# The low parts of the weights in the first block's two mixers: from GpSimd and VectorE to VectorE alone

## The chip, the cores and the metric

The kernel runs on one core of one Trainium2 chip. The metric is the device time of one execution in microseconds (us); lower is better. Engines are named as the profile does: PE is TensorE, DVE is VectorE, ACT is ScalarE, POOL is GpSimd, SP is SyncE, from which the loads are issued.

## The reference

Two transformer blocks of two layers each run one after the other over 256 tokens of width 1024, in float32. The change lies in the first block, whose two layers each have a mixer (attention, gated linear attention, a convolution branch) and a feed-forward part. In layer 0 the mixer runs over 512 columns (the context and the latent tokens), in layer 1 over the 256 latent tokens for most of its projections. Cut to what matters:

```python
def _latent_mixer(h, mem, cos, sin, p):
    proj = h @ p['w_in']                       # 9760 columns: k v kg vg glr | q qg r glu gates
    ...
    o_att = _attend_blocks(_apply_rope(q, cos, sin), k_all, v_all)
    o_gla, _, _ = _gla_bidir(qg, kg, vg, gf, gb, s_f, s_b)
    return _merge(o_att, o_gla, r, glu, gates, p)

def _conv_module(glu, p):                      # depthwise, 31 taps, over 1024 channels
    a, g = jnp.split(glu, 2, axis=-1)
    y = a * jax.nn.sigmoid(g)
    y = lax.conv_general_dilated(y, p['conv_w_dw'], ...) + p['conv_b_dw']
    y = jax.nn.silu(_layernorm(y, p['conv_ln_g'], p['conv_ln_b']))
    return y @ p['w_conv_o']

def _merge(o_att, o_gla, r, glu, gates, p):
    y_att = o_att... @ p['w_att_o']
    y_gla = (rmsnorm(o_gla) * jax.nn.silu(r)) @ p['w_gla_o']
    y_conv = _conv_module(glu, p)
    g_att, g_gla, g_conv = jnp.split(jax.nn.sigmoid(gates), 3, axis=-1)
    return (g_att * y_att + g_gla * y_gla + g_conv * y_conv) @ p['w_out']
```

## The kernel before

**Products in three matmuls.** Weights and activations are float32; the matmuls run on a shorter type. Each operand is split into a high part (the value rounded to that type) and a low part (the value minus the high part), and a product is the sum of three matmuls: high x high, low x high, high x low. For weights `wsplit` does this, tile by tile: ACT casts the loaded tile `raw` to `whi` (L362), and one elementwise subtraction gives `wlo` (recorded at L288, the line of the helper `tt`). A tile is 128 x 1024 values: eight k steps of 128 output columns (`fm`, used by `mm_fm`, L386 to L388), or two k steps of 512 columns (`proj_tm`, used by `mm_tm`, L467 to L469). The third matmul of a k step in `mm_fm` (L388), the second in `mm_tm` (L468), reads `wlo`. `whi` and `wlo` have three buffers each, `raw` two.

**Who subtracts.** `wsplit` counts its calls and sends the subtraction to POOL on every `self.pool_lo`-th call, otherwise to DVE; 0 means always DVE:

```python
on_pool = self.pool_lo and self.nsplit % self.pool_lo == 0
after = self.lo_behind.pop() if self.lo_behind else None
with self.tc.issue_after(after.ins) if after else nullcontext():
    self.tt(lo, src, hi.bitcast(F32), ALU.subtract, self.nc.gpsimd if on_pool else None)
```

`mixer` sets `pool_lo` at its start from `PLO0` (layer 0) or `PLO1` (layer 1), first entry, and again behind the attention's output projection, second entry. The second entries are 0 already. So the first entry rules: the conv branch's projections `a` and `g`, the projections k/v, q, the gate rank `glr`, kg, qg, in layer 1 also vg, and the first merge (its gates and `w_att_o`). `opening` (the first tiles of `a` and `g`), `post`, `hold` and `prehold` choose POOL by rules of their own.

**What runs beside it.** The convolution is 30 `scalar_tensor_tensor` operations on DVE for each of eight channel tiles, after one `tensor_scalar` (`conv`, tiles `ca`, L291): over both layers 480. They are generated in the background, in pairs of channel tiles, at 1.6 (layer 0) or 1.0 (layer 1) steps of four operations per weight tile, and with priority `CP` = 600, behind everything else, while the split of a weight tile has -100 (`WP`). Their sums `cs` are added up on POOL. The result is first read by `conv_norm`, at the head of the second merge. DVE also multiplies the conv gate (`gt`), normalises q and k heads (`qn`, `ra`, `rb`), and does the softmax's maximum and scaling and the low parts of activations (`s`, `P`, `PT`, `lo`); POOL raises small tiles to the power -1/2 (`s`).

**Order.** A planner orders the instructions of every engine ahead of time by priority and readiness; on the chip each engine runs its own list in order.

Of the kernel before, what the change touches and what calls it, by code (L numbers as in the profile page):

```python
# [28 lines left out]
GRATE0 = 0.8  # L29
GRATE1 = 0.6  # L30
CP = 600
PLO0A = 1
PLO0B = 0
PLO0 = PLO0A, PLO0B
PLO1A = 2
PLO1B = 0
PLO1 = PLO1A, PLO1B
NW = 8
# [2144 lines left out]
```

## Time and profile before

| | |
|---|---|
| runs | 2651.34, 2652.18, 2655.23 us; median 2652.18 us |
| profiled execution | 2647.99 us, of it 2646.2 us span |
| PE busy | 2442.5 us (92%) |
| DVE busy | 1710.3 us (65%) |
| ACT busy | 1118.7 us (42%) |
| POOL busy | 786.7 us (30%) |
| low parts of weights on DVE, on POOL | 357, 115 |

The profile is of one execution. A busy share is an average over stages; a stage is read from its own windows. "idle before, releaser" says how long an engine stood before an instruction and whose end released it. Matmuls are pipelined: their durations overlap, and starts tell the pace. The granted clock is TensorE's, as a share of 2.4 GHz.

### The profile page before, as it was taken

What the parts mean: (1) busy time and instruction counts of PE and PEld (TensorE: products, weight loads), DVE (VectorE), ACT (ScalarE), POOL (GpSimd) and SP (SyncE); (2) the same over time, 40 slices, a digit from 0 to 9 for tenths busy, and PEclk for the clock granted to TensorE, in tenths of its full rate; (3) what the DMA queues carried; (4) which work ended last, traced back from release to release, by engine and by line L of the source; (5) the groups of instructions that cost most, each with busy time, mean ns of one, the idle gap of its engine ahead of it and who ended that gap; (6) DMA issues with size and microseconds to landing.
All of it is one profiled execution on the core that took longest, in us unless ns stands there. A gap on an engine that the chain in (4) does not pass through costs nothing. (4 is left out here: it accounts for less than half of the span.)

```text
span 2646.2 us, 38822 instructions
## 1 busy us (share of the span) xinstructions
PE 2442.5 (92%) x15227; PEld 2089.7 (79%) x15227; DVE 1710.3 (65%) x2803; ACT 1118.7 (42%) x2063; POOL 786.7 (30%) x554
## 2 busy tenths in 40 slices
PE   7768889989999899999987998898999999999998
PEld 5556678777887777876886888887997989888997
DVE  5768997898345733343699879967654556546664
ACT  3113336644343422122343574554453544446443
POOL 2775531577002400101543125714035010112001
PEclk9889899999999999999989999999999999999999
DMA  7323211222334245355243224444574446653454
GB/s 245 128 70 114 64 52 48 80 65 80 112 128 159 85 142 188 113 190 199 83 125 98 67 88 123 132 138 140 175 241 127 128 131 207 202 160 101 148 185 157
DMA packets 277690, 345.41 MB, mean 131 GB/s; under 512 B 12894, under 2 KB 208888, under 8 KB 277508
## 3 DMA queue, kind: packets, MB, share of 16 engines
q1 hardware_dynamic: 277508, 342.94, 40.1%
q8 instruction: 120, 1.97, 0.3%
q14 instruction: 62, 0.51, 0.1%
HBM read 341.85 MB, written 1.05 MB: 130 GB/s over the span
## 5 line engine op out<-in xcount | busy, mean ns | idle before, releaser
L388 PE MATMUL pm<-hi,wlo 128*128 128x256 f32 (+1 forms) x2824 | 912.6, 324 | 31.7 <-POOL wlo L288 17.8
L386 PE MATMUL pm<-hi,whi 128*128 128x256 f32 (+1 forms) x2824 | 921.6, 328 | 11.8 <-ACT whi L362 4.2
L387 PE MATMUL pm<-lo,whi 128*128 128x256 f32 (+1 forms) x2824 | 915.2, 325 | 2.4 <-DVE lo L288 1.4
L362 ACT CAST whi<-raw 128x1024 fp32r<-128x1024 f32 (+1 forms) x464 | 484.7, 1048 | 895.0 <-PE pm L387 518.4
L288 DVE TENSOR_TENSOR wlo<-raw,whi 128x1024 fp32r<-128x1024 f32 (+1 forms) x357 | 452.3, 1270 | 355.7 <-ACT whi L362 355.3
L388 PEld LDWEIGHTS pm<-hi,wlo 128*128 128x128 f32 x2824 | 543.7, 193 | 75.3 <-POOL wlo L288 19.5
L386 PEld LDWEIGHTS pm<-hi,whi 128*128 128x128 f32 x2824 | 542.9, 193 | 55.8 <-ACT whi L362 6.7
L387 PEld LDWEIGHTS pm<-lo,whi 128*128 128x128 f32 x2824 | 544.4, 193 | 50.1 <-issue 7.4
L288 POOL TENSOR_TENSOR wlo<-raw,whi 128x1024 fp32r<-128x1024 f32 (+2 forms) x115 | 353.6, 3085 | 419.8 <-ACT whi L362 386.0
L291 DVE SCALAR_TENSOR_TENSOR ca<-gt,cw,ca 128x482 f32<-128x482 f32 (+29 forms) x480 | 331.6, 746 | 0.0
L468 PE MATMUL pm<-wlo,hi 128*128 128x512 f32 x536 | 216.1, 403 | 25.1 <-POOL wlo L288 25.1
L467 PE MATMUL pm<-whi,hi 128*128 128x512 f32 x536 | 217.3, 405 | 13.2 <-ACT whi L362 6.5
L469 PE MATMUL pm<-whi,lo 128*128 128x512 f32 x536 | 214.2, 400 | 0.0
L288 POOL TENSOR_TENSOR hl<-hr,hh 128x512 fp32r<-128x512 f32 (+1 forms) x38 | 54.8, 1444 | 470.1 <-ACT hh L454 321.4
L288 POOL TENSOR_TENSOR s<-s,mhalf 128x1 f32<-128x1 f32 (+2 forms) x82 | 68.1, 831 | 378.8 <-DVE s L295 375.2
L468 PEld LDWEIGHTS pm<-wlo,hi 128*128 128x128 f32 x536 | 103.9, 194 | 49.7 <-POOL wlo L288 28.2
L467 PEld LDWEIGHTS pm<-whi,hi 128*128 128x128 f32 x536 | 104.1, 194 | 39.8 <-ACT whi L362 7.3
L469 PEld LDWEIGHTS pm<-whi,lo 128*128 128x128 f32 x536 | 103.8, 194 | 22.2 <-DVE lo L291 0.4
L288 POOL TENSOR_TENSOR hl<-raw,hh 128x512 fp32r<-128x512 f32 x24 | 35.9, 1515 | 234.5 <-ACT hh L432 232.2
L288 POOL TENSOR_TENSOR eq<-B 128x256 f32<-128x256 f32 x96 | 89.7, 953 | 28.8 <-DVE lo L288 15.9
L467 PE MATMUL pm<-hh,hi 128*128 128x512 f32 (+2 forms) x258 | 92.6, 362 | 5.9 <-ACT hh L432 3.3
L288 POOL TENSOR_TENSOR ek<-B 128x256 f32<-128x256 f32 (+1 forms) x100 | 95.6, 975 | 3.9 <-PE ps L1209 2.0
(327 smaller groups left out, 3470.8 us busy)
## 6 DMA issues: line engine op xcount, KB each, us to landing
raw<-in_w_in_dram SPq DMA_DIRECT2D x84, 1024.0 KB
aw<-in_w_ada_dram SPq DMA_DIRECT2D x192, 256.0 KB
raw<-in_w_gate_up_dram SPq DMA_DIRECT2D x40, 1024.0 KB
raw<-in_w_ff_gate_dram SPq DMA_DIRECT2D x21, 1024.0 KB
raw<-in_w_ff_up_dram SPq DMA_DIRECT2D x21, 1024.0 KB
raw<-in_w_down_dram SPq DMA_DIRECT2D x20, 1024.0 KB
raw<-in_w_ff_down_dram SPq DMA_DIRECT2D x18, 1024.0 KB
raw<-in_w_att_o_dram SPq DMA_DIRECT2D x8, 1024.0 KB
```

Source lines behind the costliest of these rows:

```text
L288: return (eng or self.nc.vector).tensor_tensor(out=out, in0=a, in1=b, op=op)
L291: return self.nc.vector.scalar_tensor_tensor(out=out, in0=a, scalar=s, in1=b, op0=op0, op1=op1)
L362: self.nc.scalar.copy(hi, src)
L386: mm(out, lhsT=hi[:, k, :], rhs=a.hi[k], start=(first and k == 0), stop=False)
L387: mm(out, lhsT=hi[:, k, :], rhs=a.lo[k], start=False, stop=False)
L388: mm(out, lhsT=lo[:, k, :], rhs=a.hi[k], start=False, stop=(last and k == nk - 1))
L467: f(p, lhsT=a.hi[kk][:, sl], rhs=hi, start=first, stop=False)
L468: f(p, lhsT=a.hi[kk][:, sl], rhs=lo, start=False, stop=False)
L469: return f(p, lhsT=a.lo[kk][:, sl], rhs=hi, start=False, stop=last)
```

## The change

Two constants. In the first part of layer 0's mixer every weight tile had its low part made by POOL, in that of layer 1 every second one; now DVE makes all of them.

```diff
-PLO0A = 1
+PLO0A = 0
 PLO0B = 0
 PLO0 = PLO0A, PLO0B
-PLO1A = 2
+PLO1A = 0
 PLO1B = 0
 PLO1 = PLO1A, PLO1B
```

## Rows read from the trace of the kernel before

**Rows 1.** The page, span in 40 slices (tenths): PE busy, granted clock.

```profile
PE   7768889989999899999987998898999999999998
...
PEclk9889899999999999999989999999999999999999
```

**Rows 2.** Waits of PE from 53 to 482 us: total, times, longest.

```profile
PE pm L468 <- POOL wlo L288: 22.3, 3, 16.3
PE pm L388 <- POOL wlo L288: 15.3, 2, 12.9
```

**Rows 3.** Windows behind these waits: length, busy PE PEld DVE ACT POOL, granted clock.

```profile
110.60:114.60 4.00, 3.97 (x9) 3.13 (x10) 0.00 (x0) 0.00 (x0) 4.00 (x2) 0.50 0.75 212
170.00:176.00 6.00, 6.00 (x14) 4.74 (x15) 0.00 (x0) 0.00 (x0) 4.55 (x2) 0.50 0.44 132
90.40:97.00 6.60, 6.60 (x22) 5.28 (x23) 6.60 (x11) 0.00 (x0) 6.60 (x1) 0.74 0.00 0
196.60:199.00 2.40, 2.40 (x6) 1.92 (x7) 0.00 (x0) 0.00 (x0) 2.40 (x2) 0.50 0.52 113
```

**Rows 4.** Timeline of POOL, low parts in mixer 0: start, us.

```profile
118.73 2.39 POOL L288 TENSOR_TENSOR wlo<-raw,whi 128x1024 fp32r<-128x1024 f32 x1 [3.50 <-ACT whi L362]
124.18 2.39 POOL L288 TENSOR_TENSOR wlo<-raw,whi 128x1024 fp32r<-128x1024 f32 x1 [3.05 <-ACT whi L362]
...
75.56 14.78 POOL L288 TENSOR_TENSOR wlo<-raw,whi 128x1024 fp32r<-128x1024 f32 x1 [4.93 <-ACT whi L362]
...
90.30 20.28 POOL L288 TENSOR_TENSOR wlo<-raw,whi 128x1024 fp32r<-128x1024 f32 x1
...
142.61 27.29 POOL L288 TENSOR_TENSOR wlo<-raw,whi 128x1024 fp32r<-128x1024 f32 x1 [2.40 <-ACT whi L362]
...
340.42 2.39 POOL L288 TENSOR_TENSOR wlo<-raw,whi 128x1024 fp32r<-128x1024 f32 x1 [7.86 <-ACT whi L362]
```

**Rows 5.** Timeline of DVE, convolution taps in mixer 0 and mixer 1.

```profile
71.30 16.83 DVE L291 SCALAR_TENSOR_TENSOR ca<-gt,cw,ca 128x482 f32<-128x482 f32 x26
88.05 2.84 DVE L288 TENSOR_TENSOR adar<-adar,ab 4x512 f32<-4x512 f32 x1
...
340.50 2.85 DVE L291 SCALAR_TENSOR_TENSOR ca<-gt,cw,ca 128x500 f32<-128x500 f32 x1
...
1384.96 8.18 DVE L291 SCALAR_TENSOR_TENSOR ca<-gt,cw,ca 128x241 f32<-128x241 f32 x21
```

**Rows 6.** POOL's low parts by line, 53 to 482 us and 1310 to 1625 us.

```profile
L288 POOL TENSOR_TENSOR wlo<-raw,whi 128x1024 fp32r<-128x1024 f32 (+1 forms) x49 | 188.8, 3866 | 185.7 <-ACT whi L362 175.3 <-PE pm L388 10.3
...
L288 POOL TENSOR_TENSOR wlo<-raw,whi 128x1024 fp32r<-128x1024 f32 (+1 forms) x29 | 78.7, 2713 | 133.2 <-ACT whi L362 117.3 <-DMA raw<-in_w_att_o_dram 7.9 <-ACT hTh L302 5.9
```

**Rows 7.** DVE by line: 53 to 482 us, then 1310 to 1650 us.

```profile
L291 DVE SCALAR_TENSOR_TENSOR ca<-gt,cw,ca 128x482 f32<-128x482 f32 (+14 forms) x240 | 193.5, 861 | 0.0
...
L291 DVE SCALAR_TENSOR_TENSOR ca<-gt,cw,ca 128x241 f32<-128x241 f32 (+14 forms) x240 | 138.1, 631 | 0.0
L288 DVE TENSOR_TENSOR wlo<-raw,whi 128x1024 fp32r<-128x1024 f32 x36 | 44.4, 1234 | 11.3 <-ACT whi L362 11.3
```

**Rows 8.** Windows of mixer 0's first part: busy PE PEld DVE ACT POOL, clock.

```profile
53.00:188.00 135.00, 99.50 (x426) 75.33 (x425) 88.98 (x123) 26.20 (x37) 93.87 (x17) 0.85 0.33 108
188.00:300.00 112.00, 90.54 (x376) 67.85 (x375) 92.94 (x144) 32.09 (x110) 61.04 (x28) 0.88 0.27 87
300.00:410.00 110.00, 98.32 (x513) 83.80 (x512) 98.52 (x155) 40.22 (x92) 41.97 (x17) 0.97 0.19 58
```

**Rows 9.** Timeline of DVE: mixer 0's last tap, the first use of the sums.

```profile
386.97 1.75 DVE L291 SCALAR_TENSOR_TENSOR ca<-gt,cw,ca 128x482 f32<-128x482 f32 x1
...
496.81 3.07 DVE L288 TENSOR_TENSOR ca<-ca,ps 128x512 f32<-128x512 f32 x5
```

**Rows 10.** Waits of PE from 1310 to 1650 us (mixer 1, first part).

```profile
PE pm L388 <- DVE wlo L288: 11.9, 4, 4.9
...
PE pm L388 <- POOL wlo L288: 2.6, 3, 1.8
```

**Rows 11.** DVE's low parts from 482 to 760 us: min/median/max ns.

```profile
L288 DVE TENSOR_TENSOR wlo<-raw,whi x39: 1199/1225/1673, 485.4 to 755.3; 128x1024 fp32r<-128x1024 f32 x39
```

## The prediction

> **What bounds the kernel now.** I read the page first. TensorE is busy for most of the span, and its slices stand at 8 or 9 almost everywhere; the weak ones are among the first eight, where the granted clock dips to 8 as well [rows 1]. That is the first part of mixer 0, where all low parts are POOL's. So I asked for TensorE's waits between 53 and 482 us, from the first of these low parts to the last. The two longest entries by far are matmuls that wait for a `wlo` made by POOL: 22.3 us at L468 and 15.3 us at L388, 37.6 us together [rows 2]. The windows behind these waits show the second cost: TensorE comes back at a granted clock of 0.50 (1.2 GHz) and stays there for some microseconds [rows 3].
>
> Why is POOL late? Alone, one 128x1024 low part takes it 2.39 us, and two follow each other at 5.45 us, TensorE's pace for one 128-column weight tile, as the first two rows of [rows 4] show. But other ones of the same form last 14.78, 20.28 and 27.29 us [rows 4]. VectorE's timeline shows what runs beside the first of these: 26 convolution taps back to back, 71.3 to 88.1 us [rows 5]. POOL's instruction is issued at 75.56 and ends at 90.34, 2.2 us after the chain, about what it needs alone, and VectorE's next instruction, a small addition, lasts 2.84 us meanwhile; under the chain POOL made no visible progress. The reverse is in the rows too: a tap that meets a POOL low part issued just before it (340.42) takes 2.85 us [rows 5], against 16.83 / 26 = 0.65 in the chain. So POOL and VectorE exclude each other here, and a chain without gaps keeps POOL out to its end. In total 49 low parts of mixer 0 cost POOL 188.8 us where 49 x 2.39 = 117 would do, and the 29 of mixer 1 cost 78.7 [rows 6].
>
> The Trainium skill ("SBUF — State Buffer", section "Who interferes with whom") states that a VectorE instruction with two SBUF inputs and a GpSimd instruction that reads SBUF take turns by an exclusive lock held for a whole instruction. The 2.85 us tap agrees. Read as a lock of one instruction only, it would have POOL wait one tap (0.65) and end after about 3 us; the 27.29 us row says otherwise, and by that reading the 37.6 us below would not be there to gain. The sum goes by the rows.
>
> **The change part by part.**
>
> *Removed, mixer 0.* POOL's 49 low parts up to `self.pool_lo = ...[1]`. TensorE's waits for them: 37.6 us [rows 2]. The clock behind them: 4.0 + 6.0 + 2.4 us at 0.50 lose half, 6.2 us, and 6.6 us at 0.74 lose 0.26 of it, 1.7 us [rows 3]; 7.9 in all. Together 45.5 us. These waits end the idle of TensorE itself, and right after them TensorE runs without a gap, so I count them in full.
>
> *Added, mixer 0.* 49 low parts on VectorE at 1.23 us (the mean of the 36 that VectorE makes in and just behind mixer 1 [rows 7]): 60 us of VectorE. What hides them? VectorE is busy 89.0 + 92.9 + 98.5 = 280.4 us of the 357 us from 53 to 410 [rows 8]. It also loses what the exclusion costs: the 240 taps take 193.5 us [rows 7], 240 x 0.65 = 156 without POOL, so 37.5 us come back, up to what POOL's few remaining operations there still take. 280.4 + 60.3 - 37.5 = 303 us, in a stretch that shrinks to 357 - 45.5 = 311.5. It fits, with little to spare, and the taps may slip: the last one ends near 388 and the first instruction that needs the finished sums runs at 496.8 [rows 9], so over 100 us of cover, some 60 after the stage has shrunk.
>
> *The price of the new neighbours.* VectorE's queue is in order: a low part now stands behind whatever taps, gate products, head norms or softmax steps were placed ahead of it, and what waits for it is a later matmul of the same k step, with all of TensorE behind. Before shows this on both sides. In mixer 1, where VectorE makes half of them beside the taps, TensorE waits 11.9 us for them [rows 10], over 36 [rows 7]: 0.33 us each, 16 us for 49. In the second part of mixer 0 VectorE makes 39 [rows 11] with no taps beside them, and no wait of TensorE names them: 0. Mixer 0's first part has the taps of the former, but the 512-column matmuls, and so the double cover per weight tile, of the latter. I take the middle, 8 us, and keep 0 and 16 for the range.
>
> *Mixer 1.* 29 low parts leave POOL: 2.6 us of TensorE's waits go [rows 10]. VectorE gets 29 x 1.23 = 35.7 us more, and gives up the tap time lost to POOL: 138.1 - 240 x 0.39 (8.18 / 21 [rows 5]) = 44.5 us. That nearly cancels. By 0.33 us each the new low parts would cost TensorE 9.6 us; but the old ones were themselves late behind VectorE work that POOL held up. Between -15 (both kinds of wait gone) and +7 (9.6 less 2.6) I take 0.
>
> *Not touched.* ScalarE still makes all high parts, the DMA queue issues the same loads from SP, `post`, `hold` and `prehold` set POOL by themselves. POOL keeps the conv sums and the small powers, and finds its way free for them.
>
> *Sum.* -45.5 + 8 + 0 = -37.5 us on the profiled execution's 2648.0 us, 2610.5. That execution lies 4.2 us under the median of the three runs, 2652.2; on the median the forecast is **2614.7, say 2615 us**.
>
> **Rivals.**
>
> *Long chains ahead of a low part (slower).* If the order on VectorE puts chains such as the 26 taps of [rows 5] ahead of a `wlo`, the stall is only moved. There are three `wlo` buffers, one in use, so a low part can be two weight tiles ahead: 2 x 5.45 = 10.9 us of cover, 17 taps. A 26-tap chain of 16.83 us overruns it by 5.9 us, plus some 2.5 us of low clock: 8.4 each. Two such chains for each of the four tap pairs make 67 us, 2652 - 45.5 + 67 = 2674. It decides from six chains on (6 x 8.4 = 50). For it: VectorE's chains are that long now. Against: the taps are given a priority 700 steps behind the low parts, and enter the program at 1.6 x 4 = 6.4 per weight tile, 4.2 us. Chance 0.11.
>
> *VectorE becomes the bound.* If the exclusion gives nothing back (POOL's other work meets the taps as often), the stage holds 280.4 + 60.3 = 341 us of VectorE against 311.5 us of TensorE, and 29 of the 45.5 us are lost: 2652 - 16 = 2636. For it: VectorE is busy 98.5 of 110 us from 300 to 410 [rows 8]. Against: 49 of the POOL operations that meet the taps are the ones that go. The Trainium skill ("Perfetto Trace Analysis", section "Optimizing Scalar/DVE Operations") has the rule on this side, that a saturated VectorE may hand work even to GpSimd, and adds that the two share a port, so that it might not help; [rows 5] speak for the second half. Chance 0.13.
>
> *Mixer 1 gains too.* VectorE loses there 44.5 us to POOL and gets 35.7; if TensorE's 11.9 us for late low parts shrink with the POOL operations that held VectorE, and mixer 0's new waits stay near 0, another 8 (new waits) and 9 us or so (mixer 1) go: about 2598. Chance 0.13.
>
> *The stall only changes its name.* TensorE, no longer held by POOL, meets the taps, the head norms or the softmax at the same places, and the stage ends when it ended: 2652. Against: the waits of [rows 2] are ended by POOL alone, and the taps have 100 us in hand. Chance 0.05.
>
> **How the numbers follow.** The forecast, 2603 to 2632, has 0.58 (its own bounds: 0 and 16 for the new waits, and some microseconds either way for mixer 1). A measurement of this kernel tells about 0.2%, 5.3 us, from no change. Forecast, mixer 1 and VectorE-bound lie below that: 0.84 faster; 0.05 the same; 0.11 slower. The range 2594 to 2645 leaves out about 0.05 below, and the no-change and slower cases, 0.16, above.
>
> **What the profile after would show.** Right: no `wlo` on POOL between 53 and the end of mixer 0's first part, no TensorE wait there of over 10 us, clock 9 or more in the first eight slices, 49 and 29 more low parts on VectorE at about 1.2 us, taps at a mean near 0.7 in place of 0.86, and this stage about 40 us shorter with the rest of the kernel unchanged in length. Wrong: waits of TensorE for `wlo` from VectorE over 20 us (chains), a VectorE without gaps and conv sums finished late, so that TensorE waits at the head of the `w_conv_o` stage (bound), or equal waits under other names.

## The result and the profile after

The changed kernel takes 2571.38 us (median of 4, 2570.36 to 2573.77) against 2653.7 us for the kernel before measured beside it: a ratio of 0.9686, 95% interval 0.9665 to 0.9708. It gains 82 us where 38 were forecast, and lies 23 us under the low end of the range. The sign was right, the size was not.

The profiled execution after has a span of 2569.3 us. On the page, the busy tenths and the granted clock in 40 slices, which answer to [rows 1]:

```profile
PE   7989899899999999998999997899998999999998
...
DVE  5998987995355533343799888866635655546564
...
POOL 1011001792014100003310005632062100112001
PEclk9989999999999999999999998999999999999999
```

POOL is nearly empty in the first seven slices (to 450 us, behind mixer 0's first part), TensorE stands higher there, and the clock has one 8 left. To see how much of the change lies where, I cut both traces at the same instructions: mixer 0's stage from 53 us to the first matmul on the finished convolution sums (L1349), mixer 1's from the last transpose of a tap matrix (L1313) to the last matmul on its sums (L1349). Windows of these two stages, the kernel before (from, to, length, busy time of PE, PEld, DVE, ACT and POOL with counts, granted clock, DMA):

```profile
53.00:492.60 439.60, 370.94 (x1753) 296.73 (x1752) 341.61 (x539) 160.43 (x337) 216.87 (x71) 0.91 0.25 80
1330.50:1627.50 297.00, 258.66 (x1662) 235.09 (x1662) 261.69 (x476) 147.33 (x268) 92.17 (x50) 0.94 0.32 98
```

The same windows after:

```profile
53.00:435.50 382.50, 355.39 (x1756) 288.22 (x1755) 341.74 (x588) 161.00 (x337) 29.02 (x22) 0.97 0.29 92
1273.00:1549.00 276.00, 257.80 (x1738) 237.36 (x1737) 248.43 (x506) 152.01 (x276) 26.14 (x25) 0.98 0.37 114
```

Mixer 0 is 57.1 us shorter and mixer 1 21.0, together 78.1 of the 76.9 us between the two spans; the rest of the kernel keeps its length to about 1 us. In mixer 0 TensorE's idle time falls from 439.6 - 370.9 = 68.7 us to 27.1, and its busy time, for the same matmuls, by 15.5 us, as the mean clock goes from 0.91 to 0.97. Notice VectorE: it has 588 instructions for 539, the 49 low parts, and is busy for the same 341.7 us, in a stage that is 57 us shorter.

TensorE's waits after, first in mixer 0 (53 to 435.5 us), then in mixer 1 (1273 to 1549 us), for [rows 2, 10]: engine, line, what it waits for, sum, times, longest.

```profile
PE pm L468 <- DVE wlo L288: 9.2, 1, 9.2
PE ps L995 <- ACT PT L302: 8.2, 4, 3.8
PE ps L915 <- DVE ra L288: 1.6, 1, 1.6
...
PE pm L467 <- DVE qn L288: 4.0, 3, 1.5
...
PE pm L388 <- DVE wlo L288: 2.1, 2, 1.6
...
PE ps L915 <- DVE ra L288: 1.5, 3, 0.6
```

The kernel before, in the same two stages, had these beside the waits for POOL. They were in the list when I predicted, and I passed them over:

```profile
PE ps L915 <- DVE ra L288: 5.9, 2, 5.6
PE ps L995 <- ACT PT L302: 5.8, 2, 3.0
PE ps L969 <- DVE P L295: 4.9, 2, 3.3
...
PE pm L388 <- DVE wlo L288: 11.9, 4, 4.9
PE ps L915 <- DVE ra L288: 8.4, 6, 2.3
PE pm L467 <- ACT whi L362: 6.2, 1, 6.2
```

Waits for POOL's `wlo` are gone, and most of those on VectorE and ScalarE have shrunk too: in mixer 1 `wlo` made by VectorE from 11.9 to 2.1 us and `ra` from 8.4 to 1.5, although VectorE makes some 30 low parts more there. Not all have: mixer 0 has a new one of 9.2 us for a `wlo`, and the one for `PT` goes from 5.8 to 8.2. VectorE by line after, mixer 0 (53 to 425 us) and mixer 1 (1252 to 1572 us), for [rows 7]:

```profile
L291 DVE SCALAR_TENSOR_TENSOR ca<-gt,cw,ca 128x482 f32<-128x482 f32 (+14 forms) x240 | 160.9, 723 | 0.0
L288 DVE TENSOR_TENSOR wlo<-raw,whi 128x1024 fp32r<-128x1024 f32 (+1 forms) x49 | 59.0, 1209 | 2.2 <-ACT whi L362 2.2
...
L291 DVE SCALAR_TENSOR_TENSOR ca<-gt,cw,ca 128x241 f32<-128x241 f32 (+14 forms) x240 | 103.5, 481 | 0.0
L288 DVE TENSOR_TENSOR wlo<-raw,whi 128x1024 fp32r<-128x1024 f32 x66 | 80.7, 1225 | 9.6 <-ACT whi L362 9.4
```

The taps have fallen from 193.5 to 160.9 and from 138.1 to 103.5 us. The 9.2 us stall is the long chain ahead of a low part, seen once. VectorE's timeline there (start, us):

```profile
169.92 12.24 DVE L291 SCALAR_TENSOR_TENSOR ca<-gt,cw,ca 128x500 f32<-128x500 f32 x19
182.08 1.48 DVE L295 TENSOR_SCALAR ca<-gt,cw,vt 128x512 f32<-128x512 f32 x1
183.49 1.74 DVE L288 TENSOR_TENSOR adar<-adar,ab 4x512 f32<-4x512 f32 x1
185.15 0.53 DVE L295 TENSOR_SCALAR ca<-gt,cw,vt 128x512 f32<-128x512 f32 x1
185.61 1.33 DVE L291 SCALAR_TENSOR_TENSOR ca<-gt,cw,ca 128x482 f32<-128x482 f32 x2
186.87 2.34 DVE L288 TENSOR_TENSOR wlo<-raw,whi 128x1024 fp32r<-128x1024 f32 x2
```

And TensorE's timeline behind it; the bracket is the idle time before the matmul and what ended it:

```profile
188.13 0.80 PE L468 MATMUL pm<-wlo,hi 128*128 128x512 f32 x1 [9.22 <-DVE wlo L288]
```

### The profile page after: what moved, and what is told of

Same layout as the page of the kernel before. It is cut to its first block, busy times and chain, and to the rows that moved or that the text cites. A ratio compares the mean times of both kernels' runs of the same rounds, so it can differ in the third digit from the quotient of the medians.

```text
span 2569.3 us, 38799 instructions
## 1 busy us (share of the span) xinstructions
PE 2422.1 (94%) x15227; PEld 2079.7 (81%) x15227; DVE 1694.9 (66%) x2883; ACT 1117.6 (43%) x2063; POOL 522.0 (20%) x474
## 5 line engine op out<-in xcount | busy, mean ns | idle before, releaser
L288 DVE TENSOR_TENSOR wlo<-raw,whi 128x1024 fp32r<-128x1024 f32 (+2 forms) x437 | 547.9, 1257 | 356.6 <-ACT whi L362 355.7
L386 PEld LDWEIGHTS pm<-hi,whi 128*128 128x128 f32 x2824 | 540.7, 192 | 62.5 <-ACT mt L298 10.4
L291 DVE SCALAR_TENSOR_TENSOR ca<-gt,cw,ca 128x482 f32<-128x482 f32 (+29 forms) x480 | 264.4, 602 | 0.0
L288 POOL TENSOR_TENSOR wlo<-raw,whi 128x1024 fp32r<-128x1024 f32 (+1 forms) x35 | 80.6, 2319 | 95.9 <-ACT whi L362 90.9
L468 PE MATMUL pm<-hl,hi 128*128 128x512 f32 (+2 forms) x258 | 93.2, 362 | 1.5 <-POOL hl L288 1.2
```

Source lines behind the costliest of these rows:

```text
L288: return (eng or self.nc.vector).tensor_tensor(out=out, in0=a, in1=b, op=op)
L291: return self.nc.vector.scalar_tensor_tensor(out=out, in0=a, scalar=s, in1=b, op0=op0, op1=op1)
L386: mm(out, lhsT=hi[:, k, :], rhs=a.hi[k], start=(first and k == 0), stop=False)
L468: f(p, lhsT=a.hi[kk][:, sl], rhs=lo, start=False, stop=False)
```

## The experiments

The theory formed from this profile: POOL's low parts cost TensorE twice, once where a matmul waited for one, and once because each holds up VectorE's operations that read two tensors from SBUF (two-input operations from here on: the taps, the subtractions) and so makes everything that VectorE hands to TensorE late. The rival: the gain is the removed waits and the clock behind them alone, with VectorE's time hidden, as the prediction had it. Twelve kernels ran. "Mixer 0" and "mixer 1" are the lengths of the two stages defined above, from each kernel's profile; the kernel before stood at 2651.7 to 2654.2 us beside them.

| kernel | us (median) | ratio to before [95%] | mixer 0 | mixer 1 |
|---|---|---|---|---|
| before | 2653.7 | | 439.6 | 297.0 |
| after | 2571.38 | 0.9686 [0.9665, 0.9708] | 382.5 | 276.0 |
| e1 change in mixer 0 only | 2599.12 | 0.9792 [0.975, 0.9835] | 383.3 | 299.9 |
| e2 change in mixer 1 only | 2629.04 | 0.9911 [0.9883, 0.994] | 443.9 | 277.1 |
| e4 half of mixer 0, all of mixer 1 | 2591.56 | 0.9769 [0.9719, 0.9818] | 403.4 | 277.0 |
| e3 after, POOL busy unawaited | 2664.29 | 1.0046 [1.0025, 1.0068] | 439.4 | 309.9 |
| e5 low parts not made | 2524.65 | 0.9513 [0.9495, 0.9531] | 352.9 | 257.5 |
| e6 e5, POOL busy unawaited | 2590.22 | 0.9762 [0.974, 0.9785] | 393.7 | 286.0 |
| e9 e5, POOL busy writing | 2532.04 | 0.954 [0.9519, 0.956] | 360.0 | 261.9 |
| e10 e5, VectorE busy unawaited | 2566.32 | 0.9665 [0.9645, 0.9686] | 379.3 | 276.2 |
| e7 after, `post` on VectorE | 2570.54 | 0.9687 [0.9667, 0.9707] | 384.1 | 277.3 |
| e8 e7, `hold` and `prehold` on VectorE | 2561.85 | 0.9651 [0.963, 0.9671] | 384.1 | 277.9 |
| e11 e8, fewer taps, layer 0 | 2566.4 | 0.9674 [0.9655, 0.9692] | 390.5 | 277.0 |
| e12 e11, fewer taps, layer 1 too | 2571.94 | 0.969 [0.9673, 0.9706] | 390.8 | 284.5 |

### One mixer at a time: e1, e2, e4

Against the kernel after, e1 has `PLO1A = 2` back, e2 has `PLO0A = 1` back, and e4 gives POOL every second low part of mixer 0:

```
e1:  -PLO1A = 0   +PLO1A = 2
e2:  -PLO0A = 0   +PLO0A = 1
e4:  -PLO0A = 0   +PLO0A = 2
```

> Only layer 0's mixer has its low parts on VectorE; layer 1's keeps every second one on POOL. The traces put 57 us of the gain before the convolution norm of mixer 0 and 21 us into mixer 1. If the two parts are independent: 2653.7 - 57 = about 2596 us. If mixer 1's gain only came from mixer 0's other timing: about 2574.

> Only layer 1's mixer has them on VectorE. Independent parts: 2653.7 - 21 = about 2632 us. By the recorded forecast, in which the dearer VectorE and the lighter POOL cancel in mixer 1: 2653. If mixer 1 owes nothing to the change itself: 2653 as well.

> Layer 0's mixer has every second low part on POOL, layer 1's none. Theory 1: a chain of taps keeps POOL out as before, but half as many low parts meet one, and VectorE is held up half as often: 20 to 40 us of mixer 0's 57 us are given back, 2591 to 2611. If TensorE's waits came from POOL's load (2.4 us for each 5.45 us), half the load has none left: about 2575.

e1 gains 55.1 us and e2 25.2 against the kernel before; the sum, 80.3, agrees with the 82 us of the whole change within the spread of the runs, and both kernels end within 4 us of what independent parts would give (2596 and 2632). Mixer 1 is worth some 20 to 28 us where the sum had 0, and only 2.6 us of TensorE's waits there were for POOL [rows 10]: the removed waits alone do not make this. e4 ends 20.2 us above after, at the low edge of what the first theory expected and far from the 2575 of the second, and its mixer 0 keeps 36.2 of the 57.1 us: half of the low parts give 63% of the gain.

### Is it the waiting, or POOL beside VectorE? e3

The kernel after, in which VectorE makes every low part, with 80 subtractions on POOL added whose result nobody reads, where before had its low parts. A copy of one column by ScalarE, behind the high part, starts each (code shortened):

```
         self.nc.scalar.copy(hi, src)
+        if self.ghost and self.nsplit % self.ghost == 0:   # ghost = (1, 2)[l]
+            t = self.sp.tile([128, 1], F32, tag="gh", bufs=6)
+            nc.scalar.copy(t, first column of hi)
+            self.tt(self.scr, ones_d broadcast, t broadcast, ALU.subtract, nc.gpsimd)
```

> The changed kernel, with VectorE making all low parts, and 80 additional POOL subtractions at the places where POOL made low parts before: 128x896, two SBUF inputs, started by one small ScalarE copy of each high part, result read by nobody. TensorE can never wait for them; VectorE's order is the same but for 24 of 2771 lines. Theory 1, that POOL's work also cost through VectorE, which it holds up: taps return to means near 0.8 and 0.6 us, TensorE's waits for VectorE's head norms and low parts return, the time rises by 20 to 40 us, to 2591 to 2611. Theory 2, that all of the gain is TensorE's waits for POOL and the rest is the planner's other order on VectorE: 2571 to 2577.

The whole gain is gone: 2664.29 us, 92.9 more than after and 0.46% more than before. That is the first theory's direction, but 53 us above the top of its range. Window of mixer 0 in e3:

```profile
53.00:492.40 439.40, 371.17 (x1756) 297.39 (x1755) 400.17 (x588) 166.76 (x386) 192.83 (x71) 0.93 0.25 80
```

TensorE's longest waits in it:

```profile
PE ps L1003 <- ACT PT L303: 16.8, 5, 7.1
PE pm L475 <- DVE wlo L289: 16.0, 4, 9.6
PE pm L474 <- DVE modT L296: 7.3, 1, 7.3
PE ps L923 <- DVE ra L289: 7.1, 2, 4.6
```

VectorE's taps in it, by line:

```profile
L292 DVE SCALAR_TENSOR_TENSOR ca<-gt,cw,ca 128x482 f32<-128x482 f32 (+14 forms) x240 | 195.6, 868 | 0.0
```

The stage has before's length (439.4 against 439.6 us) and before's TensorE time, without one matmul that waits for POOL's low part. That the two lengths agree is chance: before, VectorE had none of the 49 low parts to make, and here it has all of them. The taps are back at 195.6 us, VectorE has gone from 341.7 to 400.2 us, and the stage has grown by 56.9, nearly what VectorE grew (58.4). TensorE now waits for `wlo`, `modT` (scales and shifts of a norm) and `ra`, which VectorE makes, and for `PT`, which ScalarE copies behind VectorE's softmax steps. POOL's own queue is not the way: VectorE's only waits for POOL in mixer 0 are for the small powers of the head norms, and they are the same after and in e3:

```profile
DVE qn L288 <- POOL s L288: 9.6, 12, 0.9
...
DVE qn L289 <- POOL s L289: 9.6, 12, 0.9
```

So POOL's operations cost TensorE time without being waited for, and the rival that counts the removed waits alone falls.

### The prices one by one: e5, e6, e9, e10

e5 leaves out the 80 moved low parts, 49 in mixer 0 and 31 in mixer 1 (the matmuls read the high part in their place), so it has neither price:

```
+        if self.skip and self.nsplit % self.skip == 0:     # skip = (1, 2)[l]
+            return hi, hi
```

e6 is e5 with e3's unawaited subtractions on POOL. e9 is e5 with, per low part, one subtraction of a single column on POOL and two memsets of 128x896 that only write:

```
+            self.tt(self.scr[:, 0:1], ones_d[:, 0:1], t, ALU.subtract, nc.gpsimd)
+            for _ in range(2):
+                nc.gpsimd.memset(self.scr, 0.0)
```

e10 is e6 with the big subtraction on VectorE (`None` in place of `nc.gpsimd`).

> The 80 low parts that the change moves are not made at all; the matmuls that would read them read the high part again, so the output is not the reference's and the instruction count of TensorE is kept. It has neither the price on POOL nor the price on VectorE. By the recorded forecast's own price for the new neighbours, 8 us: changed kernel - 8 = about 2563 us. If the 95 us of VectorE's new work stood on TensorE's path to a good part: 2520 to 2550.

> As the kernel without these low parts, with the 80 unawaited POOL subtractions (128x896, started by a small ScalarE copy each). VectorE has no low part of these to make, TensorE waits for none, POOL is as busy as before the change. Theory 1, POOL's work holds VectorE and through it TensorE also where VectorE makes no low parts: 20 to 35 us above the kernel without low parts. Theory 2, the holding costs only where VectorE is full of low parts as well: within 5 us of it.

> As the kernel without these 80 low parts, and behind each high part POOL does one subtraction of a single column, which ties it to that place, and two memsets of 128x896 (no SBUF input), read by nobody. POOL is busy and late as with the unawaited subtractions, but reads SBUF only for a moment. Theory 1, what costs is that POOL's reads and VectorE's two-input operations exclude each other: most of the 66 us of the unawaited subtractions are gone, 2525 to 2545. Theory 2, what costs is POOL's own queue, in which the small powers of the head norms stand behind the long subtractions: the price stays, 2570 to 2590.

> As the kernel without these 80 low parts, and VectorE does the unawaited 128x896 subtractions in place of POOL (about 1.0 us each, 80 us in all). Theory 1, VectorE's time is itself nearly the bound in the two mixers, so that work there costs whether or not TensorE waits for it: 30 to 45 us above 2524.65, like the 47 us that the real low parts cost. Theory 2, the 47 us are TensorE waiting for the low parts themselves (late behind chains of taps): at most 10 us above.

Windows of mixer 0 and mixer 1 in e5:

```profile
53.00:405.90 352.90, 346.04 (x1754) 281.94 (x1753) 286.13 (x539) 160.71 (x337) 26.70 (x22) 1.00 0.31 100
1242.20:1499.70 257.50, 246.94 (x1663) 226.96 (x1663) 216.39 (x476) 147.20 (x268) 20.69 (x24) 0.99 0.36 113
```

With none of the 49 low parts to make, TensorE idles 352.9 - 346.0 = 6.9 us in mixer 0, at full clock. Of the 68.7 us of idle time before, 62 hung on the low parts, not the 37.6 that name them. The 2524.65 us lie in the range of new work on TensorE's path, not at the 2563 of the forecast's own price.

*VectorE's own price.* After lies 46.7 us above e5 (29.6 in mixer 0, 18.5 in mixer 1) for 80 low parts of 1.22 us, 98 us of VectorE. e10, whose subtractions nobody waits for and which are a little shorter (some 88 us of VectorE, 54.9 of them in mixer 0), lies 41.7 us above e5, as its first theory had it. So most of that price is not a wait for a low part; it is VectorE's time. TensorE's longest wait in e10's mixer 0:

```profile
PE pm L476 <- DVE qn L289: 9.8, 2, 9.2
```

The one stall of 9.2 us that after has on a `wlo` is here, as long and at nearly the same place, one on `qn`, a head norm, with no `wlo` there to be late.

*POOL's price.* e6 lies 65.6 us above e5 (40.8 and 28.5 in the two stages), about twice the top of what its first theory expected. Not all of this is exclusion. Window of its mixer 0:

```profile
53.00:446.70 393.70, 356.51 (x1755) 289.17 (x1754) 322.60 (x539) 167.13 (x386) 181.68 (x71) 0.96 0.28 90
```

POOL's timeline in it:

```profile
63.07 1.68 POOL L289 TENSOR_TENSOR scr<-ones_d,gh 128x896 bf16<-128x896 f32 x1 [4.83 <-ACT gh L368]
...
88.11 2.72 POOL L289 TENSOR_TENSOR scr<-ones_d,gh 128x896 bf16<-128x896 f32 x1 [5.87 <-ACT gh L368]
93.56 65.06 POOL L289 TENSOR_TENSOR scr<-ones_d,gh 128x896 bf16<-128x896 f32 x4 [2.73 <-ACT gh L368]
...
172.61 0.71 POOL L289 TENSOR_TENSOR s<-s,mhalf 128x2 f32<-128x2 f32 x1
```

ScalarE's waits for POOL in e6, and the end of TensorE's longest stall:

```profile
ACT gh L368 <- POOL scr L289: 12.7, 3, 10.4
...
173.93 0.77 PE L476 MATMUL pm<-whi,hi 128*128 128x512 f32 x1 [16.35 <-DVE qn L289]
```

Four subtractions take 65 us under VectorE's chains, the six small `gh` buffers, into which ScalarE copies its columns, run out, and ScalarE, which makes the high parts, waits 10.4 us for one; then the power operation `s` of a head norm stands behind the rest of them in POOL's queue until 172.6, and `qn` with it. TensorE's one stall of 16.3 us ends there. So part of e6 is the experiment's own: without that stall, and before what the low clock behind it cost, 24.5 us of mixer 0's 40.8 are left. e3 has no such wait of ScalarE, and its 92.9 us stand without it. That they are more than e6's because VectorE is fuller there is likely, but not tried by itself.

*Occupied or reading?* e9 keeps POOL nearly as busy (167.4 us of mixer 0 against 181.7 in e6) and costs 7.4 us in all, the small ScalarE copies included; 2532.04 us is where its first theory put it. POOL by line in its mixer 0:

```profile
L371 POOL MEMSET scr<- 128x896 bf16 x98 | 83.3, 850 | 5.6
L289 POOL TENSOR_TENSOR scr<-ones_d,gh 128x1 bf16<-128x1 f32 x49 | 58.1, 1186 | 159.9 <-ACT gh L368 158.8
```

VectorE's taps in mixer 0 of e5, e9 and e6, in this order:

```profile
L292 DVE SCALAR_TENSOR_TENSOR ca<-gt,cw,ca 128x482 f32<-128x482 f32 (+14 forms) x240 | 162.7, 734 | 0.0
...
L292 DVE SCALAR_TENSOR_TENSOR ca<-gt,cw,ca 128x482 f32<-128x482 f32 (+14 forms) x240 | 162.6, 734 | 0.0
...
L292 DVE SCALAR_TENSOR_TENSOR ca<-gt,cw,ca 128x482 f32<-128x482 f32 (+14 forms) x240 | 186.5, 830 | 0.0
```

POOL's writing costs the taps nothing, its reading 24 us. The Trainium skill ("SBUF — State Buffer", section "Who interferes with whom") says so: a VectorE instruction with two SBUF inputs contends with a GpSimd instruction that reads SBUF and not with one that only writes it; the taps of these runs agree.

### Going on: e7, e8, e11, e12

If POOL's reads cost more than the work costs VectorE, the other ones should go as well. e7 moves `post`'s low parts of the first block to VectorE; e8 also those that `hold` and `prehold` make; e11 and e12 then put fewer taps on each weight tile, so that VectorE's chains are shorter:

```
e7:  -pool_lo, self.pool_lo = self.pool_lo, 1
     +pool_lo, self.pool_lo = self.pool_lo, 0
e8:  -... self.nc.gpsimd if k % 2 else None      +... None    (hold)
     -... self.nc.gpsimd if i % 2 else None      +... None    (prehold)
e11: -CRATE0 = 1.6    +CRATE0 = 1.2
e12: -CRATE1 = 1.0    +CRATE1 = 0.75
```

> The changed kernel, and in addition the low parts of the weights in the output projections behind the mixers and feed-forward parts (post, 31 on POOL) are VectorE's. There VectorE is idle beside them and some of POOL's stand in the chain that ended last, at 2.4 us each. If the chain through the loads shortens by the 1.2 us that VectorE saves on each of the some 14 in it: 5 to 17 us faster, 2554 to 2566. If the loads set that stage: the same.

> As before it, and hold and prehold also give every low part to VectorE, so that POOL makes no low part of a weight behind the opening. If POOL is dearer wherever VectorE works beside it: faster than the one with post alone, 2545 to 2560. If two engines side by side are better where tiles are made in a burst ahead of the held matmuls: slower than it by 3 to 15 us.

> The version in which POOL makes no low part of a weight behind the opening, with the convolution of layer 0 generated at 1.2 in place of 1.6 steps per weight tile. The trace after shows one stall of 9.2 us for a low part behind 19 taps, and low clock behind it. If fewer taps per tile take that stall away: 2561.85 - 12 = about 2550. If the taps only move behind the attention and delay the convolution norm, or the planner fills VectorE all the same: 2560 to 2575.

> As before it, and layer 1's convolution at 0.75 in place of 1.0. If tap density is what delays low parts and head norms there too: 3 to 8 us faster than with layer 0's rate alone; if the taps just end later, where the convolution norm waits for them: slower by 2 to 10 us.

e7 changes nothing that can be told (2570.54 against 2571.38), so the 5 to 17 us did not come. e8 gains 8.7 us more: its runs (2557.5 to 2563.6) lie wholly below e7's (2568.5 to 2574.2), so 2561.85 us is the best version of the study, some 90 us under before. Its two mixers have e7's length; the gain lies elsewhere. The two profiled executions show 4.9 us of it, 3.8 by the last matmul of L1914, in the second block (2288.0 us against 2291.8 in e7). Fewer taps per weight tile only lose, as the second expectation of each had it: against e8, mixer 0 is 6.4 us longer in e11, mixer 1 6.6 longer in e12; the whole kernel's 4.6 us between e8 and e11 are not clear of the spread of the runs. In e11 TensorE then waits for the sums themselves, 8.3 us at L1349, and still 7.6 us for a `wlo`:

```profile
PE ps L1349 <- POOL cs L288: 8.3, 1, 8.3
PE pm L468 <- DVE wlo L288: 7.6, 1, 7.6
```

## Why the prediction was right in sign and wrong in size

*Mixer 0, the waits for POOL and the clock behind them, -45.5.* The 37.6 us of waits went in full. The clock was mis-sized: TensorE's busy time fell by 15.5 us, where the four stretches behind the named waits [rows 3] made 7.9; the other 7.6 us lie outside of those stretches.

*The new neighbours, +8.* As a wait for `wlo` the number was met, in part by luck: 8 was the middle between 0 and 16, and what came is one stall of 9.2 us with 19 taps ahead of it. That is the rival of long chains, which had priced 8.4 us for each chain and feared eight; one came. As the price of the low parts on VectorE it was far too small: 29.6 us in mixer 0 (after against e5) and 18.5 in mixer 1, nearly all of it there when nobody waits for them (e10).

*The exclusion, lifted: 0. This is the step that failed.* I had the mechanism, and its size on the taps (-37.5 forecast, -32.6 measured; mixer 1 -44.5 and -34.6), though not that VectorE's other operations were held too: its busy time in mixer 0 took 49 low parts of 59.0 us without growing, so 59 us came back. And then I asked only whether VectorE's time "fits", 303 of 311.5 us, and priced everything that fits at nothing. The runs show no such threshold. In mixer 0 VectorE's 286, 323, 342 and 400 us (e5, e6, after, e3) go with stages of 353, 394, 383 and 439: VectorE's added time shows in the stage well below the point where it would fill it. For low parts on VectorE it is about half (29.6 of 55.6 us, e5 to after; 26.4 of 48.4, e5 to e10), for POOL's reads more: nearly all beside a full VectorE (56.9 of 58.4, after to e3), about two thirds in e6 without its own stall (24.5 of 36.5). VectorE's total alone doesn't tell the stage: before and after have the same 342 us of it and lie 57.1 us apart. The cover of 100 us behind the last tap [rows 9] covers the taps, not the softmax, the head norms and the low parts that stand in VectorE's queue between them, and for those TensorE waits a little, many times. The row that would have told was in the list of waits: idle time of 68.7 us, of which POOL's `wlo` names 37.6; the largest of the other 31.1 name `ra`, `PT` and `P`, 16.6 us (10.6 after). After, 27.1 us of idle less the new 9.2 leave 17.9: 13.2 us of those other waits went. So mixer 0 is -37.6 - 15.5 - 13.2 + 9.2 = -57.1. That the 13.2 went with POOL's reads is read from e3, where such waits come back; the split itself is an account of one trace against another.

*Mixer 1, 0.* The same step: I let 35.7 us of new VectorE work cancel 44.5 us given back, microsecond for microsecond. VectorE did get about that (80.7 - 44.4 = 36.3 us of low parts), the taps gave back 34.6, and the stage is 21.0 us shorter. (31 low parts left POOL in mixer 1; 29 is what the recorded window held.) This is the rival "Mixer 1 gains too", whose mechanism came true (waits for VectorE's `wlo` from 11.9 to 2.1 us) at more than its 9 us; `ra` and one `whi`, 6.9 and 6.2 us, came on top.

*The rivals.* "The stall only changes its name" and "VectorE becomes the bound" did not happen; e3 makes the second one's condition (POOL meets the taps as often, and VectorE makes the low parts) and gives 2664 us, not 2636. Again the fit was the wrong measure: VectorE is busy 400 of 439 us there, not without a gap.

*What stays open.* Before lies 86.7 us above e5 in mixer 0. How much of this is waiting for POOL and how much is POOL's reads beside VectorE can't be told sharply: e6 says 45.9 and 40.8, and without its own 16.3 us stall 62.2 and 24.5. The two prices also don't add: e3 lies 139.6 us above e5, after and e6 46.7 and 65.6, together 112.3. That VectorE's lateness is what TensorE feels in e3 is read from the names of its waits, from the unchanged waits for POOL's powers and from e9, not tried by itself. Why low parts on VectorE cost the stage half of their time and not all is argued, from the gaps that VectorE has left, and not shown.

## What to carry to other kernels

An engine that hands many small results to the bound engine is not free until it is full: price each microsecond added to it or taken from it at a share of the bound engine's time (here about a half for work of its own, two thirds to nearly all for time lost to POOL's reads), and read the small waits in the list, not only the largest. Before giving an elementwise operation to POOL, count what its reads do to VectorE's two-input operations: here POOL made 80 subtractions at a cost of 127 us of the kernel (before against e5), VectorE at 47. To find such a price, run the suspect operation with nobody waiting for it, with every buffer that starts it deep enough, and beside it the same engine busy in a way that leaves out the suspected conflict.

## What the hardware showed that was not expected

POOL's read stays out for as long as VectorE's chain of two-input operations goes on, not for one instruction: four subtractions in e6, of a kind that took 1.68 to 2.72 us each in the 30 us before them, took 65.06 us. A small read fares the same: of the 49 subtractions of a single column in e9's mixer 0, the median took 0.2 us, and one, beside such a chain, 16.3 us. And work that nobody waits for still held TensorE through its engine's queue: a 0.71 us power operation behind starved subtractions, with ScalarE out of buffers ahead of it, stood at the end of a stall of 16.3 us.
